# Prompt attention of an NSA step on one core: scores in plain fp32, two heads on the halves of the rows, keys and values kept on chip

## The chip, the core and the metric

The kernel runs on one core of a Trainium2 chip. The metric is device time in microseconds (us); it is given as the median of three runs. The engines are called by the profile's names: PE is TensorE (PEld its weight loads), DVE is VectorE, ACT is ScalarE, POOL is GpSimd, and SP is SyncE, which here only issues DMAs. Each engine has its own queue and takes its instructions in the order of the program.

## What is computed

The program is one inference step of a small decoder trunk: a gated short-convolution layer, then one layer of native sparse attention (NSA) with three branches (compressed, selected, window), then the output projection. It does this for a prompt of 512 new tokens, and for 8 sample rows of one new token each, which read 2,048 cached tokens per row by pages. There are 16 heads of 64, in 4 groups of 4 that share keys and values (4 KV heads). For each query and each branch:

```python
def masked_softmax(s, mask):
    s = jnp.where(mask, s, NEG)
    e = jnp.exp(s - jnp.max(s, axis=-1, keepdims=True)) * mask
    return e / jnp.maximum(jnp.sum(e, axis=-1, keepdims=True), 1e-30)
...
p_win = masked_softmax(scores(qg, win_kv[:, 0], 'qhgd,nhd->qhgn'), w_mask[:, None, None, :])
o_win = jnp.einsum('qhgn,nhd->qhgd', p_win.astype(q.dtype), win_kv[:, 1])
...
o = g[..., 0:1] * o_cmp + g[..., 1:2] * o_sel + g[..., 2:3] * o_win
```

For the prompt all 512 keys of the selected and of the window branch are scored under a causal mask (in tiles of 128 queries, so that query tile qt sees 128·(qt+1) keys), and 32 compressed keys besides. The output o is multiplied by a gate z and projected with a 1024x1024 matrix.

## The kernel before

The program runs in stages on the one core. To 650 us it computes the convolution layer, while PE is busy nearly all the time. Then come the shared keys and values (to 692), the queries (`q_steps`, with the compression of the prompt's keys, to 752), the gates z and the key and value projections (`kvz_steps`), mixed with the key side of the sample rows (to 934), and the attention (935 to 1192), with a tail to 1202.

**The attention.** `attention` (L926) draws steps from two generators. `prompt_steps` (L956) runs over 16 tiles (kvh, qt): 4 KV heads by 4 query tiles. For each tile `prompt_scores` (L1004) makes the scores, their masked maximum (a DVE reduce, L1050), the exponential (ACT, L1053) and a scaling by gate over sum (POOL, L1068), and `prompt_values` (L1076) transposes the probabilities on PE (L1110), evicts them by ACT (L1114) or DVE (L1112) into `pt`, and multiplies by the values (L1101). The second generator, `side`, is the value half of the sample rows (`sample_values`, matmuls at L1335): per page of 128 cached tokens it needs 128 KB, which SP fetches with a register load (L1372) and a DMA (L1377), into two rings of buffers named `kt` and `skv`; 128 pages and some larger loads in all (window rows L1395, `vc_scratch` L1342). When the tiles of the last KV head begin (`last_head`), what is left of `side` is emitted, and from there the output projection (`out_steps`, matmuls L114 to L116, and L1460/L1461 for the sample rows) takes its place. This sets only the order in which the program is written. A scheduler that simulates the engines then moves instructions within it, so PE's final order is its result; the order of SP's queue is fixed by hand.

**Number formats.** A product of two fp32 numbers is made in three fp32r passes (high by high, high by low, low by high) in most stages, so operands are split into a high and a low part. In `q_steps` each head's query is split by one ACT copy (L896) and one DVE subtraction (L897) into QA or QB [128, 2, 4, 512], where the two halves of the 128 rows hold high and low parts. The scores of one head are two accumulated fp32r matmuls over 128 rows (L1043) against KK, which holds a key and its copy on both row halves, high and low as two planes.

**Keys and values on the way.** `kv_prep` (L799) makes, for each branch and KV head, a doubled copy `kd` of the keys (POOL, L805), 4 transposes (L809), a split, and a 512 KB write to `kk_scratch` in DRAM (POOL's queue, L812); the values go to `vt_scratch` (L816). `prompt_head` (L990) loads them again per KV head: VA once (L999, 1 MB), KK for each head (L1002, 1 MB), and copies the 32 compressed keys into place (L1001).

**PSUM.** Eight banks: transposes draw from a ring of two pairs (`tr` and `tx`, two buffers each), the scores have `s` with two buffers, and `acc0` and `acc1` take sums. For the output projection `acc1` and the `tx` pair are used in turn (`psum_o`, L1399).

Of the kernel before, what the change touches and what calls it, by code (L numbers as in the profile page):

```python
# [18 lines left out]
KT = 8  # L19
# [59 lines left out]
class Yoco:  # L79
# [480 lines left out]
    def w1_prep(self):  # L560
# [29 lines left out]
        self.KKd = nc.dram_tensor("kk_scratch", (4, 128, 2, 1024), F32, kind="Internal").ap()  # L590
        self.VTd = nc.dram_tensor("vt_scratch", (128, 2, 1024), F32, kind="Internal").ap()
# [33 lines left out]
    def compress_tail(self, acc, c, n, b):  # L625
# [18 lines left out]
        if c == 0:  # L644
# [4 lines left out]
            if b is None:  # L649
                self.split(self.KC[:, 0], self.KC[:, 1], p3)  # L650
            else:
                kc = cp.tile([128, 2, 128], F32, name="kc", bufs=1)
                for o in range(2):
                    nc.scalar.activation(kc[o * 64:(o + 1) * 64],
                                         p3[o * 64:(o + 1) * 64].rearrange("p (a o) n -> p a o n", o=2)[:, :, o, :],
                                         AF.Copy)
                nc.sync.dma_start(self.KCd[b], kc)
        else:
# [4 lines left out]
            if b is None:  # L663
                p3 = ps[:n, :256].rearrange("p (h d) -> p h d", d=64)

                nc.vector.tensor_copy(self.VC[0:32], p3)
                for o in range(1, 4):
                    nc.gpsimd.tensor_copy(self.VC[o * 32:o * 32 + 32], self.VC[0:32])
# [6 lines left out]
    def kv_init(self):  # L675
# [3 lines left out]
        self.VC = self.slot("VC", [128, 4, 64], F32, "kx1")  # L679
        self.KC = self.slot("KC", [128, 2, 4, 32], F32R, "kx2")  # L680
# [35 lines left out]
    def kv_work(self, br, c, wt):  # L716
# [10 lines left out]
        else:  # L727
            CD = self.kvp.tile([128, 4, 256], F32, name="kvt", bufs=2)
# [70 lines left out]
    def kv_prep(self, br, c, kvt):  # L799

        nc = self.nc
        if c == 0:
            for kvh in range(4):
                kd = self.kvp.tile([128, 4, 2, 64], F32, name="kd", bufs=1)
                nc.gpsimd.tensor_copy(kd, kvt[:, :, kvh * 64:kvh * 64 + 64][:, :, None, :].to_broadcast([128, 4, 2, 64]))  # L805
                yield
                ps = self.psum1()
                for t in range(4):
                    nc.tensor.transpose(ps[:, t * 128:(t + 1) * 128], kd[:, t].rearrange("p u d -> p (u d)"), self.ident)  # L809
                st = self.kvp.tile([128, 2, 512], F32R, name="st", bufs=2)  # L810
                self.split(st[:, 0], st[:, 1], ps)
                nc.gpsimd.dma_start(dram(self.KKd, kvh * 128 * 2048 + (2 - br) * 512, [[2048, 128], [1024, 2], [1, 512]]),  # L812
                                    st.bitcast(F32))
                yield
        else:
            nc.gpsimd.dma_start(self.VTd[:, br - 1], kvt.rearrange("p t n -> p (t n)"))  # L816
            yield
# [56 lines left out]
    def q_steps(self):  # L874
        nc = self.nc
        I = self.I

        QA = self.hp.tile([128, 2, 4, NT], F32R, name="QA", tag="hT")
        QB = self.slot("QB", [128, 2, 4, NT], F32R, "gr1")
        self.QK = [QA[:, 0], QA[:, 1], QB[:, 0], QB[:, 1]]  # L880
        self.QS = self.keep.tile([128, KT, NS], F32, name="QS")
        two = lambda ap: ap.rearrange("p (a n) -> p a n", a=2)
        for hp in range(2):
            for gp in range(2):
                wt = self.wsplit(self.qz_load(0, hp, gp), "norm_b")
                for g2 in range(2):
                    ps = yield from self.product(wt, g2, 128)
                    g = gp * 2 + g2
                    q = self.slot("q", [128, T], F32, "kx%d" % (3 + g2))
                    nc.vector.tensor_tensor(two(q), ps, two(self.RB), op=ALU.mult)  # L890
                    nc.gpsimd.tensor_copy(self.QS[:, hp * 4 + g, :], q[:, NT:])
                    for h2 in range(2):
                        a = slice(h2 * 64, h2 * 64 + 64)
                        o = slice(64 - h2 * 64, 128 - h2 * 64)
                        QK = self.QK[hp * 2 + h2]
# [57 lines left out]
    def psum_s(self):  # L953
        return self.px.tile([128, 512], F32, name="s", bufs=2)

    def prompt_steps(self):  # L956

        tiles = [(kvh, qt) for kvh in range(4) for qt in QORD]
        prev = None
        self.done = []  # L960
        heads = {}
        ahead = self.prompt_head(0, heads)
        for i, (kvh, qt) in enumerate(tiles):
            if qt == QORD[0]:

                for _ in ahead:
                    yield
                self.last_head = kvh == 3
            elif qt == QORD[1] and kvh < 3:
                ahead = self.prompt_head(kvh + 1, heads)  # L970
            H = heads[kvh]
            P = []
            scores = self.prompt_scores(H, kvh, qt, P)
            if prev:

                acc = 0
                for k, _ in enumerate(self.prompt_values(*prev)):
                    acc += SF * 4 / (2 * tiles[i - 1][1] + 3)
# [3 lines left out]
                    if k % 2 and qt != QORD[0]:  # L982
                        next(ahead, None)
# [3 lines left out]
            prev = (heads[kvh], kvh, qt, P)  # L987
# [3 lines left out]
    def prompt_head(self, kvh, heads):  # L991
        nc = self.nc
        at = self.pr

        KK = at.tile([128, 2, 1056], F32R, name="KK", bufs=2)
        heads[kvh] = KK
        if kvh == 0:
            self.VA = at.tile([128, 2, 4, 256], F32, name="VA")
# [4 lines left out]
        yield  # L1003

    def prompt_scores(self, H, kvh, qt, P):
        nc = self.nc
        at = self.pr
        KK = H
# [4 lines left out]
        QK = self.QK[kvh][:, :, qs]  # L1013
        st = at.tile([128, 3, 4, 3], F32, name="pst", bufs=2)
        mx, l, f = st[:, 0], st[:, 1], st[:, 2]
        PC = at.tile([128, 4, 32], F32, name="PC", bufs=3)
        apart = qt in CA
        if apart:
            psc = self.psum1()
            for g in range(4):  # L1020
                for s in range(2):
                    nc.tensor.matmul(psc[:, g * 32:g * 32 + 32], QK[:, g], KK[:, s, 0:32], start=s == 0, stop=s == 1)
            for g in range(4):
                nc.vector.tensor_tensor_reduce(out=PC[:, g], in0=psc[:, g * 32:g * 32 + 32], in1=CM, scale=-SCALE,
                                               scalar=1e28, op0=ALU.add, op1=ALU.min, accum_out=mx[:, g, 0:1])
        for g in range(4):
            pw = self.psum_s()
            ranges = []
            if apart:
                win = pw[:, :W]  # L1030
                ranges += [(win, slice(32, 32 + W))]
            else:
                win, cmp_ = pw[:, 32:32 + W], pw[:, 0:32]
                ranges.append((pw[:, :32 + W], slice(0, 32 + W)))
# [474 lines left out]
```

## Time and profile before

| | us |
|---|---|
| median of 3 runs | 1199.39 (1198.85 to 1204.46) |
| profiled execution, its own time | 1204.16 |
| its span, first to last instruction | 1202.4 |
| PE busy in the span | 1143.7 (95%) |
| attention, 935 to 1192 | 257 |
| PE busy in 935 to 1076, of 141 | 122.8 |
| PE busy in 1076 to 1192, of 116 | 111.8 |

A stage is read by asking which wait ends last in it. A high busy share of PE over the whole span says only that most stages are bound by PE; the attention has two halves that differ, and the last matmul of the sample rows' side (1076) lies between them.

### The profile page before, as it was taken

The numbers are of one execution on the slowest core, as the hardware profiler recorded it, in microseconds if no ns is written. First come the engines' busy times: TensorE is split into PE (matmuls) and PEld (weight loads), VectorE is DVE, ScalarE is ACT, GpSimd is POOL, SyncE is SP. The second block draws the span as 40 slices with busy tenths as digits, with TensorE's granted clock in tenths as the row PEclk, the third lists the DMA queues.
The fourth block names the chain that finished last, engine by engine and source line by source line (L and its number), as shares of the span: only waits on it lengthen the run. The fifth ranks groups of instructions, "written<-read, shape, count | busy, mean of one in ns | idle before, by whom it ended". The sixth has DMA issues, their size and how long they took to land. (4 is left out here: it accounts for less than half of the span.)

```text
span 1202.4 us, 23306 instructions
## 1 busy us (share of the span) xinstructions
PE 1143.7 (95%) x9002; PEld 1023.1 (85%) x9002; DVE 645.3 (54%) x1454; ACT 548.1 (46%) x1096; POOL 266.1 (22%) x373
## 2 busy tenths in 40 slices
PE   6899999999999999999999999989899699899996
PEld 5899999999999999999999999868788455456676
DVE  5545464465544555545548376534345367676832
ACT  6344343353343533435347374433346365566631
POOL 5210310211102111012103001010100355555641
PEclk9899999999999999999999999999999799899999
DMA  7563663665435745448332624587883657665001
GB/s 204 175 195 113 196 210 108 197 198 162 141 115 158 245 132 164 126 130 267 122 124 45 176 45 132 161 271 194 248 204 102 222 172 222 186 202 219 20 36 71
DMA packets 160208, 192.71 MB, mean 160 GB/s; under 512 B 48001, under 2 KB 139497, under 8 KB 159321
## 3 DMA queue, kind: packets, MB, share of 16 engines
q1 hardware_dynamic: 122784, 125.03, 34.5%
q0 software_dynamic: 12112, 44.10, 11.1%
q10 hardware_dynamic: 25200, 22.09, 6.2%
q8 instruction: 71, 1.16, 0.4%
q14 instruction: 41, 0.33, 0.1%
HBM read 167.92 MB, written 31.70 MB: 166 GB/s over the span
## 5 line engine op out<-in xcount | busy, mean ns | idle before, releaser
L114 PE MATMUL mm<-X,wh 128*128 128x260 f32 (+1 forms) x1008 | 291.8, 290 | 3.8 <-ACT wh L103 2.7
L116 PE MATMUL mm<-X,wh 128*128 128x260 f32 (+1 forms) x1008 | 287.8, 286 | 0.5 <-DVE X L360 0.5
L115 PE MATMUL mm<-X,wl 128*128 128x260 f32 (+1 forms) x1008 | 288.1, 286 | 0.0
L114 PEld LDWEIGHTS mm<-X,wh 128*128 128x128 f32 (+1 forms) x1008 | 190.4, 189 | 7.2 <-ACT wh L103 2.9
L116 PEld LDWEIGHTS mm<-X,wh 128*128 128x128 f32 (+1 forms) x1008 | 190.5, 189 | 3.8 <-DVE X L360 0.7
L115 PEld LDWEIGHTS mm<-X,wl 128*128 128x128 f32 (+1 forms) x1008 | 190.7, 189 | 3.1
L603 POOL DMA_INDIRECT G<-in_cache_cmp_kv,cidx x64 | 63.1, 987 | 317.5 <-ACT Gp L609 163.3
L100 ACT ACTIVATE th<-tr 128x512 fp32r<-128x512 f32 x128 | 71.4, 593 | 101.7 <-PE tr L615 101.5
L101 DVE TENSOR_TENSOR tl<-tr,th 128x512 fp32r<-128x512 f32 x128 | 84.1, 683 | 50.0 <-ACT th L100 49.9
L1053 ACT ACTIVATE pp<-pp,pst 128x128 f32<-128x128 f32 (+3 forms) x128 | 70.9, 556 | 39.2 <-DVE pst L1050 37.3
L1068 POOL TENSOR_SCALAR pp<-pp,pst,gt 128x128 f32<-128x128 f32 (+3 forms) x128 | 77.1, 616 | 37.5 <-ACT pp L1053 18.6
L115 PE MATMUL mm<-X,wlx 128*128 128x260 f32 x288 | 82.2, 285 | 0.0
L114 PE MATMUL mm<-X,whx 128*128 128x260 f32 x288 | 81.9, 284 | 0.0
L116 PE MATMUL mm<-X,whx 128*128 128x260 f32 x288 | 81.9, 284 | 0.0
L615 PE MATMUL tr<-ident,Gp 128*128 128x128 f32 x512 | 70.5, 273 | 0.0
L101 DVE TENSOR_TENSOR wl<-wraw,wh 128x1024 fp32r<-128x1024 f32 x38 | 49.5, 1308 | 37.6 <-ACT wh L100 37.3
L1050 DVE CUSTOM_DVE_ANT_0 pp<-s,c_mw 128x128 f32<-128x128 f32 (+3 forms) x128 | 59.0, 484 | 14.1 <-PE s L1043 9.4
L100 ACT ACTIVATE wh<-wraw 128x1024 fp32r<-128x1024 f32 x38 | 39.9, 1056 | 51.6 <-PE mm L116 42.5
L615 PEld LDWEIGHTS tr<-ident,Gp 128*128 128x128 f32 x512 | 59.4, 141 | 1.9
L115 PEld LDWEIGHTS mm<-X,wlx 128*128 128x128 f32 x288 | 54.5, 189 | 2.0
L116 PEld LDWEIGHTS mm<-X,whx 128*128 128x128 f32 x288 | 54.7, 190 | 1.5
L114 PEld LDWEIGHTS mm<-X,whx 128*128 128x128 f32 x288 | 54.6, 190 | 1.4
(421 smaller groups left out, 2733.6 us busy)
## 6 DMA issues: line engine op xcount, KB each, us to landing
skv<-in_cache_sel_kv SPq DMA_DIRECT2D x172, 128.0 KB
wraw<-in_conv_w_in SPq DMA_DIRECT2D x16, 1024.0 KB
wrawx<-in_conv_w_in SPq DMA_DIRECT2D x16, 1024.0 KB
kt<-in_cache_sel_kv SPq DMA_DIRECT2D x84, 128.0 KB
wo<-wo_scratch SPq DMA_DIRECT2D x4, 2048.0 KB
out_win_kv_s<-in_cache_win_kv ACTq DMA_DIRECT2D x8, 1022.0 KB
wrawx<-in_conv_w_out SPq DMA_DIRECT2D x4, 1024.0 KB
wraw<-in_conv_w_out SPq DMA_DIRECT2D x4, 1024.0 KB
```

The source lines that it names most:

```text
L100: nc.scalar.activation(hi, src, AF.Copy)
L101: nc.vector.tensor_tensor(lo, src, hi.bitcast(F32), op=ALU.subtract)
L114: mm(out, sh, mh, start=first, stop=False)
L115: mm(out, sl, mh, start=False, stop=False)
L116: mm(out, sh, ml, start=False, stop=last)
L603: nc.gpsimd.indirect_dma_start(out=G.rearrange("p i c d -> p (i c d)"), out_offset=None, in_=table, in_offset=bass.IndirectOffsetOnAxis(ap ...
L615: nc.tensor.transpose(ps[:, h * 128:(h + 1) * 128], Gp[:, c * 4 + h, :], self.ident)
L1050: nc.vector.tensor_tensor_reduce(out=d, in0=src, in1=m, scale=-SCALE, scalar=1e28, op0=ALU.add, op1=ALU.min, accum_out=mx[:, g, i:i + 1])
L1053: nc.scalar.activation(d, d, AF.Exp, scale=-1.0, bias=mx[:, g, i:i + 1], accum_out=l[:, g, i:i + 1])
L1068: nc.gpsimd.tensor_scalar(P[g2][:, i, :W], P[g2][:, i, :W], f[:, g2, i + 1:i + 2], gates[:, g2, i + 1:i + 2], op0=ALU.mult, op1=ALU.mult)
```

## The change

- Queries stay in plain fp32, in one tile Q with the two heads of a pair (two KV heads, h2 = 0 and 1) on rows 0 to 63 and 64 to 127; the high and low split of Q goes, and with it the separate copy QS of the sample rows' queries.
- Keys likewise: two transposes groups per branch (one per pair of KV heads), evicted straight into KK in SBUF. The values go straight into VA in SBUF. Both scratch tensors in DRAM, their writes and their loads go.
- A step of scores is now two fp32 matmuls over 64 rows each, one per head of the pair, written behind one another (`side_by_side`), into two PSUM banks of one tile of two banks. `s` has two such tiles, four banks; the transposes' ring falls to the two buffers of `tr`.
- The 16 units are (hp, gp, qt): pair of KV heads, half of the group, query tile. Each has 4 (query) heads as before, but two of each KV head. The value products become four matmuls of 256 columns for each t instead of two of 512, the compressed values' are two of 256 columns; the merge `ot` becomes two copies and additions of 64x256 and one POOL multiply of 128x256.
- In the output projection the second and third bank in turn are the two banks of an `s` tile; all four weight tiles `wo` have buffers in one pool; `zs` has a tile of its own.

```diff
 def kv_prep(self, br, c, kvt):
-        if c == 0:
-            for kvh in range(4):
-                kd = self.kvp.tile([128, 4, 2, 64], F32, name="kd", bufs=1)
-                nc.gpsimd.tensor_copy(kd, kvt[:, :, kvh * 64:kvh * 64 + 64][:, :, None, :].to_broadcast([128, 4, 2, 64]))
...
-                nc.gpsimd.dma_start(dram(self.KKd, kvh * 128 * 2048 + (2 - br) * 512, [[2048, 128], [1024, 2], [1, 512]]),
-                                    st.bitcast(F32))
...
+        for hp in range(2):
+            ps = self.psum1()
+            for t in range(4):
+                nc.tensor.transpose(ps[:, t * 128:(t + 1) * 128], kvt[:, t, hp * 128:hp * 128 + 128], self.ident)
+            k = self.KK[:, hp, 32 + (2 - br) * 512:544 + (2 - br) * 512]
+            if hp:
+                nc.vector.tensor_copy(k, ps)
+            else:
+                nc.scalar.activation(k, ps, AF.Copy)
...
 def q_steps(self):
-                    nc.vector.tensor_tensor(two(q), ps, two(self.RB), op=ALU.mult)
-                    nc.gpsimd.tensor_copy(self.QS[:, hp * 4 + g, :], q[:, NT:])
...
-                        nc.scalar.activation(QK[a, g], q[a, :NT], AF.Copy)
-                        nc.vector.tensor_tensor(QK[o, g], q[a, :NT], QK[a, g].bitcast(F32), op=ALU.subtract)
+                    nc.vector.tensor_tensor(two(self.Q[:, hp * 4 + g, :]), ps, two(self.RB), op=ALU.mult)
...
 def attention(self, side):
-        self.ring = [(self.ps, "tr", 2), (self.px, "tx", 2)]
+        self.ring = [(self.ps, "tr", 2)]
...
 def psum_s(self):
-        return self.px.tile([128, 512], F32, name="s", bufs=2)
+        t = self.px.tile([128, 2, 512], F32, name="s", bufs=2)
+        return [t[:, 0], t[:, 1]]
...
-        tiles = [(kvh, qt) for kvh in range(4) for qt in QORD]
+        units = [(hp, gp, qt) for hp in range(2) for gp in range(2) for qt in QORD]
...
-            nc.gpsimd.dma_start(self.VA.rearrange("p b t n -> p b (t n)"), self.VTd)
-        for s in range(2):
-            nc.vector.tensor_copy(KK[:, s, 0:32], self.KC[:, s, kvh, :].bitcast(F32))
-        nc.gpsimd.dma_start(KK[:, :, 32:].bitcast(F32), self.KKd[kvh])
...
+    def side_by_side(self, todo):
+        first = None
+        for out, w, x, start, stop in todo:
+            with ExitStack() as st:
+                if first:
+                    st.enter_context(self.tc.issue_after(first.ins))
+                    st.enter_context(self.tc.high_priority())
+                m = self.nc.tensor.matmul(out, w, x, start=start, stop=stop)
+            first = first or m
...
-                for s in range(2):
-                    nc.tensor.matmul(out, QK[:, g], KK[:, s, cs], start=s == 0, stop=s == 1)
+            for h2 in (1, 0):
+                a = slice(h2 * 64, h2 * 64 + 64)
+                todo.append((outs[h2], self.Q[a, hp * 4 + gp * 2 + g2, qs], self.KK[a, hp, cs], True, True))
+            self.side_by_side(todo)
...
+                for b, h2 in ((1, 0), (0, 0), (0, 1), (1, 1)):
+                    kvh = hp * 2 + h2
+                    c = slice(h2 * 256, h2 * 256 + 256)
+                    todo.append([acc[b * 64:b * 64 + 64, c], self.VA[:, b, t, kvh * 64:kvh * 64 + 64], pt[:, b, c],
+                                 t == top and h2 == 0, False])
...
-        nc.scalar.activation(t1[a], acc[o], AF.Copy)
-        nc.vector.tensor_tensor(t1[a], acc[a], t1[a], op=ALU.add)
-        sz = self.SZ[a, hp * 4:hp * 4 + 4, qs]
-        nc.gpsimd.tensor_tensor(sz, sz, t1[a].rearrange("p (g n) -> p g n", g=4), op=ALU.mult)
+        for h2 in range(2):
...
+            nc.scalar.activation(t1[a], acc[o, c], AF.Copy)
+            nc.vector.tensor_tensor(t1[a], acc[a, c], t1[a], op=ALU.add)
+        nc.gpsimd.tensor_tensor(sz, sz, t1.rearrange("p (g n) -> p g n", g=2), op=ALU.mult)
```

The change also moves instructions on PE. In the fences a row is a line of the kernel, the operation, out<-in by the program's names, and the shape. First PE's order at the start of the attention, before: L1335 is a group of the side, L1022 and L1043 are scores of the compressed keys and of the others, L1110 a transpose of probabilities.

```order
L1335 MATMUL acc_10887<-skv,PT 32x256 x4
L1326 MATMUL tr<-ident,S 8x128
L1022 MATMUL tr<-KK,QA 128x32 x8
L1335 MATMUL acc_10887<-VN,PT 32x256 x4
L1043 MATMUL s<-KK,QA 128x160 x2
L1043 MATMUL s<-KK,QA 128x128 x2
...
L1043 MATMUL s<-KK,QA 128x256 x8
L1110 MATMUL tx<-ident,pp_10930 128x128
L1335 MATMUL acc_10887<-kt,PT 32x256 x8
```

The same place after the change, where L1327 is the side's group, L981 the scores, L1073 and L1112 transposes:

```order
L1327 MATMUL acc_10769<-skv,PT 32x256 x4
L1327 MATMUL acc_10769<-VN,PT 32x256 x4
L981 MATMUL s<-KV,Q 128x160 x2
L981 MATMUL s<-KV,Q 128x128 x2
...
L981 MATMUL s<-KV,Q 128x256 x8
L981 MATMUL s<-KV,Q 128x416 x2
L1327 MATMUL acc_10769<-kt,PT 32x256 x8
L1073 MATMUL tr<-ident,PC 128x128
L1112 MATMUL tr<-ident,pp_10806 128x128
```

The scores no longer name a tile that a DMA fills (KK is now a part of KV, written on chip), and the first `kt` group of the side stands behind more scores. The second place is the end of the side on PE, before; L1101 is a value product, and the last rows are the last group of the side and what follows it.

```order
L1101 MATMUL acc_12814<-pt,VA 64x512 x2
L1335 MATMUL acc_10887<-kt,PT 32x256 x8
L1043 MATMUL s<-KK,QB 128x384 x2
...
L1335 MATMUL acc_10887<-kt,PT 32x256 x4
L1335 MATMUL acc_10887<-skv,PT 32x256 x4
L1110 MATMUL tr<-ident,pp_12848 128x128 x2
L1043 MATMUL s<-KK,QB 128x512 x2
```

And after the change, where the last `kt` and `skv` rows are again the side's last group:

```order
L1327 MATMUL acc_10769<-kt,PT 32x256 x8
L1112 MATMUL tr<-ident,pp_12169 128x128
...
L981 MATMUL s<-KV,Q 128x256 x2
L1327 MATMUL acc_10769<-kt,PT 32x256 x4
L1327 MATMUL acc_10769<-skv,PT 32x256 x4
L981 MATMUL s<-KV,Q 128x256 x4
...
L1354 MATMUL acc_12447<-c_sel,S 128x32 x2
L981 MATMUL acc_12362<-pt,KV 64x256 x8
L1112 MATMUL tr<-ident,pp_12169 128x128
```

The side's last group has moved ahead in PE's order: behind it stood 132 transposes of probabilities (L1110) before, and 180 (L1112) now, of 320 in both; SP's queue has the same order in both.

## Rows read from the trace of the kernel before

**Rows 1.** Span and mean granted clock of the core.
```profile
core 0: 1202.4 us, clock 0.978
```

**Rows 2.** Windows: stretch, length, busy time (instructions) of PE, PEld, DVE, ACT, POOL, clock, DMA share, GB/s.
```profile
692.00:752.00 60.00, 60.00 (x516) 59.82 (x513) 42.73 (x100) 35.88 (x82) 5.25 (x17) 1.00 0.32 89
752.00:935.00 183.00, 171.67 (x1554) 149.78 (x1551) 79.92 (x169) 76.06 (x146) 12.08 (x19) 0.98 0.67 194
935.00:1076.00 141.00, 122.81 (x889) 73.45 (x891) 89.59 (x426) 78.65 (x245) 72.70 (x123) 0.90 0.67 212
1076.00:1192.00 116.00, 111.75 (x790) 87.22 (x782) 66.97 (x233) 58.23 (x169) 59.45 (x79) 0.99 0.23 88
1040.00:1046.00 6.00, 3.66 (x25) 2.38 (x26) 0.65 (x2) 0.07 (x1) 2.19 (x5) 0.50 0.73 220
```

**Rows 3.** Waits of PE in 935 to 1077: total us, times, longest.
```profile
PE s L1043 <- DMA KK<-kk_scratch: 9.7, 1, 9.7
PE acc L1335 <- DMA skv<-in_cache_sel_kv: 6.0, 3, 4.4
PE acc L1335 <- DMA kt<-in_cache_sel_kv: 1.0, 1, 1.0
PE s L1043 <- DVE pst L1065: 0.8, 1, 0.8
```

**Rows 4.** Timeline of SP's queue: start, length of the group's issues, instructions.
```profile
935.89 7.27 SPq L1377 DMA_DIRECT2D kt<-in_cache_sel_kv  x8
943.68 5.22 SPq L1377 DMA_DIRECT2D skv<-in_cache_sel_kv  x4
950.08 6.76 SPq L1377 DMA_DIRECT2D kt<-in_cache_sel_kv  x8
...
996.00 0.39 SPq L1395 DMA_DIRECT2D kt<-in_cache_win_kv  x1
...
998.10 1.17 SPq L1342 DMA_DIRECT2D skv<-vc_scratch  x1
...
1026.41 6.30 SPq L1377 DMA_DIRECT2D kt<-in_cache_sel_kv  x8
1033.23 2.87 SPq L1377 DMA_DIRECT2D skv<-in_cache_sel_kv  x4
1036.67 6.67 SPq L1377 DMA_DIRECT2D kt<-in_cache_sel_kv  x8
...
1057.07 0.94 SPq L1395 DMA_DIRECT2D kt<-in_cache_win_kv  x2
```

**Rows 5.** Chain of waits in the attention: start, us, what.
```profile
998.10 9.69 DMA skv<-vc_scratch
...
1035.76 6.54 DMA skv<-in_cache_sel_kv
1042.34 1.93 PE acc L1335 x16
...
1091.34 0.61 ACT pt L1114
...
1092.68 0.70 DVE pt L1112
```

**Rows 6.** Timeline of PE: start, us, line, tile, shape.
```profile
1074.37 1.03 PE L1101 MATMUL acc<-pt,VA 128*64 128x512 f32 x4
1075.33 0.33 PE L1110 MATMUL tx<-ident,pp 128*128 128x128 f32 x1
...
1075.70 0.64 PE L1335 MATMUL acc<-kt,PT 128*32 128x256 f32 x8
1076.15 0.61 PE L1335 MATMUL acc<-skv,PT 128*32 128x256 f32 x8
1076.70 0.44 PE L1110 MATMUL tr<-ident,pp 128*128 128x128 f32 x2
...
1079.83 0.71 PE L1043 MATMUL s<-KK,QB 128*128 128x512 f32 x2
1080.37 0.60 PE L1110 MATMUL tr<-ident,pp 128*128 128x128 f32 x4
1080.90 1.08 PE L1101 MATMUL acc<-pt,VA 128*64 128x512 f32 x4
...
1191.60 0.28 PE L115 MATMUL tx<-wo,skv 128*128 128x256 f32 x1
1191.72 0.29 PE L116 MATMUL tx<-wo,pt 128*128 128x256 f32 x1
```

**Rows 7.** Lines that go or change: engine, operation, count, ns min/median/max, first and last start.
```profile
L809 PE MATMUL tr<-ident,kd x24: 270/272/328, 778.0 to 857.9; 128*128 128x128 f32 x24
...
L809 PE MATMUL acc<-ident,kd x8: 271/272/273, 842.6 to 847.8; 128*128 128x128 f32 x8
...
L896 ACT ACTIVATE QA<-q x8: 619/628/633, 696.9 to 717.3; 64x512 fp32r<-64x512 f32 x8
...
L1137 DVE TENSOR_TENSOR ot<-acc,ot x16: 672/688/695, 969.9 to 1158.8; 64x512 f32<-64x512 f32 x16
...
L1136 ACT ACTIVATE ot<-acc x16: 577/591/597, 968.2 to 1158.2; 64x512 f32<-64x512 f32 x16
```

More of the change, by code (lines that the diff above doesn't have):

```diff
@@ L727, in kv_work @@
         else:
[L728 removed]
+            CD = self.VA[:, br - 1] if c else self.kvp.tile([128, 4, 256], F32, name="kvt", bufs=2)
             self.kvt = CD
@@ L1012, in prompt_scores @@
         CM = self.cst["cm"][:, qt * 32:qt * 32 + 32]
-        QK = self.QK[kvh][:, :, qs]
         st = at.tile([128, 3, 4, 3], F32, name="pst", bufs=2)
         mx, l, f = st[:, 0], st[:, 1], st[:, 2]
+        gates = self.gt[:, qt, hp * 24:hp * 24 + 24].rearrange("p (h g b) -> p g h b", h=2, b=3)[:, gp * 2:gp * 2 + 2]
         PC = at.tile([128, 4, 32], F32, name="PC", bufs=3)
         apart = qt in CA
-        if apart:
-            psc = self.psum1()
-            for g in range(4):
-                for s in range(2):
[L1022 to L1025, printed above, removed]
@@ new lines, in exps, with compressed @@
+        def exps(d, i, b):
+            nc.scalar.activation(d, d, AF.Exp, scale=-1.0, bias=mx[:, i, b:b + 1], accum_out=l[:, i, b:b + 1])
+        def compressed():
+            nc.gpsimd.tensor_tensor(PC, PC, mx[:, :, 0:1].to_broadcast([128, 4, 32]), op=ALU.subtract)
+            nc.scalar.activation(PC, PC, AF.Exp, scale=-1.0)
+            nc.vector.tensor_reduce(l[:, :, 0], PC, axis=AX.X, op=ALU.add)
+        if apart:
+            psc = self.psum_s()
+            for g2 in range(2):
+                pair([x[:, g2 * 32:g2 * 32 + 32] for x in psc], g2, slice(0, 32))
+            for g2 in range(2):
+                for h2 in range(2):
+                    largest(PC[:, g2 * 2 + h2], psc[h2][:, g2 * 32:g2 * 32 + 32], CM, g2 * 2 + h2, 0)
+            compressed()
@@ new lines, in prompt_scores @@
+        for g2 in range(2):
+            ii = (g2 * 2, g2 * 2 + 1)
+            ps = self.psum_s()
+            b = 0 if apart else 32
+            pair([x[:, :b + W] for x in ps], g2, slice(32 - b, 32 + W))
+            if qt < 2:
+                pair([x[:, b + W:b + 2 * W] for x in ps], g2, slice(544, 544 + W))
+                sel = [x[:, b + W:b + 2 * W] for x in ps]
+            for h2 in range(2):
+                P.append(at.tile([128, 2, 384 + 128 * (qt % 2)], F32, name="pp%d" % (qt % 2), bufs=4))
+            for h2, i in enumerate(ii):
+                largest(P[i][:, 1, :W], ps[h2][:, b:b + W], MW, i, 2)
+                exps(P[i][:, 1, :W], i, 2)
+                if not apart:
+                    largest(PC[:, i], ps[h2][:, :32], CM, i, 0)
+            yield
+            if qt >= 2:
+                sel = [x[:, :W] for x in self.psum_s()]
+                pair(sel, g2, slice(544, 544 + W))
+            for h2, i in enumerate(ii):
+                largest(P[i][:, 0, :W], sel[h2], MW, i, 1)
+                exps(P[i][:, 0, :W], i, 1)
+            if g2 == 1 and not apart:
+                compressed()
+            last = g2 == (0 if apart else 1)
+            gs = slice(ii[0], ii[1] + 1)
+            for r, b in [(gs, slice(1, 3))] + ([(slice(0, 4), slice(0, 1))] if last else []):
+                nc.vector.tensor_scalar(f[:, r, b], l[:, r, b], 1e-30, None, op0=ALU.max)
+                nc.vector.reciprocal(f[:, r, b], f[:, r, b])
+            for h2, i in enumerate(ii):
+                for b in range(2):
+                    nc.gpsimd.tensor_scalar(P[i][:, b, :W], P[i][:, b, :W], f[:, i, b + 1:b + 2],
+                                            gates[:, g2, h2, b + 1:b + 2], op0=ALU.mult, op1=ALU.mult)
+            if last:
+                f4 = f.rearrange("p (g h) b -> p g h b", g=2)[:, :, :, 0]
+                nc.vector.tensor_tensor(f4, f4, gates[:, :, :, 0], op=ALU.mult)
+                nc.gpsimd.tensor_tensor(PC, PC, f[:, :, 0:1].to_broadcast([128, 4, 32]), op=ALU.mult)
+            if g2 == 1:
@@ L1088, in burst @@
         def burst(last):
[L1090 to L1102 removed]
+            todo = []
+            for t, pt in reversed(ready):
+                for b, h2 in ((1, 0), (0, 0), (0, 1), (1, 1)):
[3 more added lines that the diff above has]
+                                 t == top and h2 == 0, False])
+            if last:
+                todo[4:4] = [[acc[h2 * 64:h2 * 64 + 64, h2 * 256:h2 * 256 + 256], self.VC[:, hp],
+                              pb[:, h2 * 256:h2 * 256 + 256], False, False] for h2 in range(2)]
+                todo[-1][4] = todo[-2][4] = True
+            self.side_by_side(todo)
             ready.clear()
```

199 lines of the change are left out of this document (62 added, 137 removed).

## The prediction

> **What bounds the kernel now.** I read the windows by stage first. In 692 to 752 PE is busy 60.00 of 60.00 us and in 752 to 935 it is busy 171.67 of 183 [rows 2]: these stages are PE's. In the attention the two halves differ. In 935 to 1076 PE works 122.81 of 141 us at a granted clock of 0.90; in 1076 to 1192 it works 111.75 of 116 at 0.99 [rows 2]. The waits of PE name the loss of the first half: 9.7 us once, for KK to come back from DRAM, and 6.0 + 1.0 us for pages of the sample rows' side [rows 3].
>
> SP's queue then tells who sets the side's pace. From 935.89 it issues pages without a pause of note: 12 pages take 1036.67 - 1026.41 = 10.26 us, 0.855 each, and the last loads begin at 1057.07 [rows 4]. The chain of waits runs through such loads more than once, up to the one that PE awaits until 1042.34 [rows 5]. But the side's last group runs on PE at 1075.70 [rows 6], 18.6 us after that last issue: at its end the side is no longer late, PE is. So both are near the bound in the first half: SP hands out pages, and PE has other work between them.
>
> **The change part by part.**
>
> *Scores.* The trace has no fp32 matmul on halves of the rows. The nearest row is a pair of value products, fp32 on halves of the columns: four records (two instructions) of 512 columns from 1074.37 to 1075.33, 0.96 us [rows 6], of which about 0.09 is the change of kind of matmul; 0.87 us for 512 columns, 1.7 ns a column, for two heads. Before, two instructions of 512 columns for one head take 1080.37 - 1079.83 = 0.54 [rows 6], some 0.22 each without the change of kind, so 0.88 for two heads. The long products cost the same; what is saved lies in those of 32 columns, which have a floor of about 0.11 each. Over the whole attention I count 46.0 us of scores before and 39.1 after. If row halves did not run side by side, each pair would cost double; both ends stay for the range, and I take the column halves' price, which is the nearest row.
>
> *Values, transposes, projection.* By counts in PE's order and these prices: values 45.0 before and 41.9 after, transposes 36.6 in both (336 at 0.109, from four between 1080.37 and 1080.90 less a change of kind, rows 6), the side 18.3 in both, the projection 51.9 in both (448 at 0.116 to 0.12, rows 6), changes of kind 123 before and 153 after, 11.3 and 14.1 us. Sum: 209.1 before, 201.9 after, so PE has 7.2 us less to do.
>
> *KK and VA stay on chip.* The wait of 9.7 us [rows 3] goes. What is late next there is the pages: the first eight are issued only from 935.89 [rows 4], since SP's queue goes through the constants first, which take their place when the last projection matmul is done. The loads of KK and VA also share the DMA engines with the first pages: eight take 7.27, four 5.22, eight 6.76 us, against 6.30, 2.87 and 6.30 later [rows 4], 3.8 us in all. These come back to SP.
>
> *Key and value preparation.* 32 transposes (24 + 8, rows 7) become 16: 16 x 0.109 = 1.7 us of PE in a stage with PE busy 94% [rows 2]; with the writes to DRAM gone I put the start of the attention 2 us earlier (0 to 6).
>
> *Queries.* 16 ACT splits of 0.628 us [rows 7] and as many on DVE go from a stage in which PE has no idle time [rows 2]: nothing. Merging `ot` takes 32 instructions of 256 columns on ACT and on DVE where 16 of 512 took 0.591 and 0.688 us [rows 7]; at most that much more again, 9.5 and 11 us spread over the 257, at least nothing. Off the path while PE has work: I take nothing, and up to 3 us for the range.
>
> *Where the order puts the side.* This decides. From the first score to the last group of the side, PE's order held 105.3 us of work before, and holds 79.6 now; behind that group it held 103.8 and now holds 122.2. The terms behind it, before: 138 transposes 15.0, scores 14.8, values 17.7, projection 51.9, 37 changes of kind 3.4, the group 1.0. After: 188 transposes 20.5, scores 17.2 (9,600 columns of pairs and a floor for the short ones), values 24.9, projection 51.8, 75 changes 6.9, the group 1.0. PE reads its queue in order, so it can't take the later work while a page is missing.
>
> When do the pages come? SP starts at 935.9 - 2 = 933.9. To the last loads it needs 1057.07 - 935.89 = 121.2 us, less 3.8 (bounds: 113.3, twice that gain, and 121.2): they are issued at 1051.3. Those are 2 MB of window rows; 2.5 MB of the same kind took from 996.00 to 1007.79 (998.10 + 9.69), 11.8 us [rows 4, 5], so 2 MB take 9.4. The last group runs at about 1060.7 (1054 to 1064.5). By its own work PE would be there at 935 + 79.6 x 1.12 = 1024, so it waits some 36 us in the stretch for pages: the 9.7 us are not gained but waited in other places.
>
> Behind it, before, 103.8 us of work took 1191.9 - 1075.7 = 116.2 us [rows 6], 1.12 times as much (waits for evictions, and the rest of the clock). With the same factor 122.2 take 136.8. PE ends at 1060.7 + 136.8 = 1197.5, against 1192.0 (1191.72 + 0.29, rows 6): 5.5 us later. The tail from there to 1202.4 [rows 1] and the 1.8 us around the span stay. The profiled execution goes from 1204.2 to 1209.7; it lies 4.8 over the median, which I take along: the median goes from 1199.4 to 1204.9.
>
> **The rivals.**
>
> *A. The side does not pace PE.* Then the savings arrive: 9.7 + 7.2 x 1.12 + 2 = 19.8 us, 1179.6. For it: the side ends 18.6 us behind SP's last issue before. Against: the spacing of SP's issues, which the change leaves as it is, and the waits for pages that PE has already before, with more work between the groups.
>
> *B. The waits are not lost.* While PE waits for pages, ACT, DVE and POOL finish what is before them, so behind the last group PE finds its inputs ready and the factor falls to 1.02: 122.2 x 1.02 = 124.6, the end at 1185.3, 6.7 us earlier, 1192.7; with T at 1054 or 1064.5 it is 1186 to 1196.5. For it: PE in 1076 to 1192 waits only 4 us outright [rows 2]. Against: the buffers of probabilities are few, so the engines can't run far ahead, and a PE that waits works slower afterwards: the clock in 1040 to 1046, behind the 4.4 us wait, is 0.50 [rows 2, 3].
>
> *C. Row halves do not run side by side as column halves do.* The 17.2 us of scores behind the last group then cost up to double: + 17.2, near 1222. The change would not do what it says. It decides from the point at which a pair of 512 columns takes over 0.95 us. No row of before speaks for or against it.
>
> The Trainium skill, "TensorE: Matmul & The Clock Gate", Part 3 (Measured speedup vs the span model) gives 3.07 times for four products on quarters of the rows, instead of 4. Applied to two halves as an estimate, a pair takes 1.30 times the ideal; that would add 17.2 x 0.30 x 1.12 = 5.8 us, so about 1211. The trace's column groups agree with full overlap rather than with this: 8 instructions of 256 columns, four at a time, from 1075.70 to 1076.70 in 1.00 us [rows 6].
>
> *D. Fewer banks.* The transposes' ring falls from four banks to two. With evictions of 0.61 and 0.70 us [rows 5] on two engines against 0.44 for four transposes, each of the 47 groups of four behind the last side group could wait 0.17: 0 to 8 us; and stretches at half clock behind the page waits 2 to 4 more: 1207 to 1217.
>
> **How the numbers follow.** My forecast has 0.50, with its own range of 1198 to 1210 (the bounds of T, and the factor at 1.10 to 1.14); A has 0.13, B 0.17, C and D together 0.20 (C at its full price 0.05). 0.5% is 6 us, about what a measurement of this kernel can tell from no change: faster is under 1193.4, slower over 1205.4. The forecast lies near that upper border: 0.30 same and 0.20 slower. A is faster, B 0.13 faster and 0.04 same, C and D slower. Together: faster 0.26, same 0.34, slower 0.40. The range leaves out A and the full price of C, under 2 in 10: 1186 to 1220.
>
> **What would show it.** PE's waits of the new trace in the first half: no KK, and instead some 30 us in many waits of the side's line for pages; SP's issues still at 0.855 us a page, ending about 1051; the last group of the side at 1054 to 1065 instead of 1075.7; behind it some 137 us to PE's end. If that group came later than 1065, or the stretch behind it took 125 us, I was wrong, by A or D for the first and by B for the second. For C, a pair of scores of 512 columns has to be near 0.87 us. What would make it wrong above all is a page stream faster than SP's issues of before show.

## The result, and the profile after

The changed kernel takes 1212.67 us (median of 7 runs, 1209.16 to 1215.55), the kernel before 1201.14 (7 runs). The ratio is 1.0091, with a 95% interval of 1.0065 to 1.0117: slower by 11 us. The forecast was 1204.9, which is 5.5 over the 1199.4 that it started from.

The windows of the changed kernel, cut where its stages end: the queries, the stage of z and the keys, the attention up to the side's last group, and from there to PE's end. Columns as in [rows 2].

```profile
692.00:752.00 60.00, 60.00 (x515) 59.75 (x513) 31.29 (x85) 26.79 (x69) 1.08 (x4) 1.00 0.33 89
752.00:927.60 175.60, 166.57 (x1530) 146.47 (x1531) 75.41 (x163) 72.51 (x140) 0.00 (x0) 0.99 0.61 172
927.60:1057.52 129.92, 99.09 (x833) 54.26 (x832) 69.16 (x346) 63.40 (x204) 54.15 (x99) 0.88 0.59 179
1057.52:1203.30 145.78, 132.80 (x1012) 99.47 (x1011) 85.75 (x320) 75.63 (x226) 65.14 (x97) 0.98 0.21 80
```

The first line bears out "nothing" for the queries: the stage is PE's, busy 60.00 of 60 us as before, though DVE, ACT and POOL have less to do there. The second ends 6.8 us earlier than before. The third is the stretch that waits: PE works 99 of 130 us. The fourth, behind the side, has 132.80 us of work where the kernel before had 111.75 in 116 [rows 2]. The waits of PE in 925 to 1100 name the third line's loss, where [rows 3] had KK:

```profile
PE acc L1327 <- DMA kt<-in_cache_sel_kv: 12.0, 5, 3.9
PE acc L1327 <- DMA skv<-in_cache_sel_kv: 11.6, 4, 4.1
PE s L981 <- DVE pst L1006: 7.1, 8, 2.0
PE acc L981 <- DVE pt L1114: 2.5, 3, 1.3
```

L1327 is the side's matmul. The timeline of SP's queue, to be held against [rows 4]:

```profile
929.10 6.36 SPq L1369 DMA_DIRECT2D kt<-in_cache_sel_kv  x8
935.97 3.04 SPq L1369 DMA_DIRECT2D skv<-in_cache_sel_kv  x4
939.60 6.72 SPq L1369 DMA_DIRECT2D kt<-in_cache_sel_kv  x8
...
1015.19 6.41 SPq L1369 DMA_DIRECT2D kt<-in_cache_sel_kv  x8
1022.12 2.86 SPq L1369 DMA_DIRECT2D skv<-in_cache_sel_kv  x4
1025.55 6.68 SPq L1369 DMA_DIRECT2D kt<-in_cache_sel_kv  x8
...
1046.53 0.94 SPq L1387 DMA_DIRECT2D kt<-in_cache_win_kv  x2
```

Twelve pages still take 1025.55 - 1015.19 = 10.36 us. From the first page to the last loads it is 1046.53 - 929.10 = 117.4 us, as forecast. The timeline of PE at the side's last group and at its own end, where [rows 6] had 1075.70 and 1191.72:

```profile
1057.52 0.64 PE L1327 MATMUL acc<-kt,PT 128*32 128x256 f32 x8
1057.98 0.61 PE L1327 MATMUL acc<-skv,PT 128*32 128x256 f32 x8
1058.53 1.13 PE L981 MATMUL s<-KV,Q 64*128 64x256 f32 x8
1059.59 1.09 PE L1112 MATMUL tr<-ident,pp 128*128 128x128 f32 x8
...
1203.43 0.28 PE L116 MATMUL s<-wo,pt 128*128 128x256 f32 x1
```

The side ends 18.2 us earlier than before, and PE 11.7 us later: 146.2 us lie between the two, where 116.3 lay before. The time went into the stretch behind the side: 20.75 us more of busy PE than before (132.80 against 112.05 from 1075.70 on), and some 9 us more of waiting.

### The profile page after: what moved, and what is told of

Read it like the earlier page. It is cut to its first block, busy times and chain, and to the rows that moved or that the text cites. A ratio compares the mean times of both kernels' runs of the same rounds, so it can differ in the third digit from the quotient of the medians.

```text
span 1212.9 us, 23500 instructions
## 1 busy us (share of the span) xinstructions
PE 1136.0 (94%) x9154; PEld 1012.6 (83%) x9154; DVE 628.3 (52%) x1440; ACT 537.3 (44%) x1093; POOL 237.3 (20%) x339
## 5 line engine op out<-in xcount | busy, mean ns | idle before, releaser
L1010 ACT ACTIVATE pp<-pp,pst 128x128 f32<-128x128 f32 (+3 forms) x128 | 70.4, 550 | 36.4 <-DVE pst L1006 34.9
L981 PE MATMUL s<-KV,Q 64*128 64x256 f32 (+6 forms) x320 | 56.2, 467 | 9.8 <-DVE pst L1006 9.5
L1112 PEld LDWEIGHTS tr<-ident,pp 128*128 128x128 f32 x320 | 35.5, 144 | 25.6 <-issue 13.6
```

Source lines behind the costliest of these rows:

```text
L981: m = self.nc.tensor.matmul(out, w, x, start=start, stop=stop)
L1010: nc.scalar.activation(d, d, AF.Exp, scale=-1.0, bias=mx[:, i, b:b + 1], accum_out=l[:, i, b:b + 1])
L1112: nc.tensor.transpose(ps[:, c:c + 128], P[i][:, b, t * 128:(t + 1) * 128], self.ident)
```

## The experiments

In the names, after_ and hold28_ are made from the changed kernel, before_ from the kernel before. Two readings were set against each other. Theory 1: the pages set when the side ends, and PE's order decides how much is left behind it. Theory 2: the new attention waits more on its banks and on DVE, wherever the side stands. The expectations count PE's work by slightly higher prices for short matmuls than the prediction did (82.9 and 125.4 us before and behind the last group in place of 79.6 and 122.2). Each ratio is against runs of the kernel before beside it (medians 1197.6 to 1201.1). The last two columns come from the profiled execution.

| kernel | us | ratio to before (95%) | last side group | behind it, us |
|---|---|---|---|---|
| before | 1201.1 | 1 | 1075.7 | 116.3 |
| changed | 1212.7 | 1.0091 (1.0065 to 1.0117) | 1057.5 | 146.2 |
| after_hold28 | 1191.8 | 0.9944 (0.9914 to 0.9974) | 1064.4 | 118.7 |
| after_hold40 | 1216.9 | 1.0160 (1.0112 to 1.0208) | 1056.4 | 148.6 |
| after_poolc | 1205.1 | 1.0058 (1.0032 to 1.0084) | 1043.4 | 152.1 |
| after_static | 1198.8 | 0.9985 (0.9955 to 1.0016) | 1015.1 | 178.3 |
| after_s4 | 1210.7 | 1.0095 (1.0067 to 1.0124) | 1052.4 | 145.2 |
| before_tr2 | 1209.0 | 1.0077 (1.0052 to 1.0101) | 1067.3 | 130.5 |
| before_nokk | 1191.6 | 0.9935 (0.9912 to 0.9959) | 1067.5 | 111.2 |
| hold28_poolc | 1187.3 | 0.9900 (0.9844 to 0.9955) | 1057.3 | 117.2 |
| before_hold28_poolc | 1191.7 | 0.9929 (0.9906 to 0.9953) | 1067.7 | 112.0 |

**The side's place alone.** In the changed kernel each group of the side is tied behind the last prompt scores written before it, and the side gets a smaller share of steps (`RV`, what each step of the prompt adds to a count that draws one step of the side when it is full).

```diff
-RV = 0.4
+RV = 0.28
 def side_by_side(self, todo):
...
             first = first or m
+        self.held = first
...
             def values(t, rhs, after=None):
-                first = after
+                first = after or getattr(self, "held", None)
+                lead = first is not after
...
-                    first = first or m
+                    if lead or not first:
+                        first, lead = m, False
```

> The changed kernel, with one thing altered: each matmul group of the sample rows' side is tied on PE behind the last prompt scores written before it, and the side's share of steps is 0.28 instead of 0.40, so that its last group stands behind 107.9 us of PE's work instead of 82.9 (by counts and measured prices), with 101.1 instead of 125.4 behind it. Theory 1 (the pages pace the side, and what PE's order leaves behind the last page is added): last side group still at 1055 to 1063, behind it 101.1 x 1.19 = 120, PE's end near 1180, time 1184 to 1197. Theory 2 (the stretch behind the side is long because of the banks and the waits for DVE, wherever the side stands): the waits come back, 1207 to 1216.

Measured: 1191.8, with the side's last group at 1064.44 (1055 to 1063 expected) and 118.7 us behind it (120 expected). The waits of PE up to that group show what became of the 24 us of page waits:

```profile
PE s L981 <- DVE pst L1007: 9.9, 8, 1.9
PE acc L1329 <- DMA kt<-in_cache_sel_kv: 1.9, 2, 1.4
PE tr L1113 <- DVE pb L1082: 1.8, 1, 1.8
PE tr L1074 <- ACT pt L1117: 1.7, 4, 0.6
PE acc L981 <- DVE pt L1115: 1.6, 3, 0.7
PE acc L1329 <- DMA skv<-in_cache_sel_kv: 0.8, 1, 0.8
```

2.7 us for pages are left. Nothing was removed from the kernel; the same work, in another order, is 21 us faster. So theory 2's forecast, that the loss comes back wherever the side stands, failed. Its waits are still there, though: L981 on DVE above, and behind the side's last group PE is idle 10.5 us of 118.7, where the kernel before has 4.2 of 116.3 and the changed kernel 13.0 of 145.8. The control has the tie with the old share.

> Control: the same tie of the side's groups to the prompt's scores, but with the share of 0.40 as in the changed kernel; 81.9 us of PE's work before the last side group and 128.1 behind it. Theory 1: as the changed kernel, 1209 to 1218. Theory 2: the same. If it were under 1200, the tie itself and not the place of the side's end would be what helps.

Measured: 1216.9, no better than without the tie, and 18.6 us of page waits again:

```profile
PE acc L1329 <- DMA kt<-in_cache_sel_kv: 16.2, 7, 4.0
...
PE acc L1329 <- DMA skv<-in_cache_sel_kv: 2.4, 1, 2.4
```

So it is not the tie: the two runs differ in the share alone, and with it in PE's order, which has 128.1 us of work behind the side's end here and 101.1 there.

**Earlier pages.** In the changed kernel SP waits 21.5 us for room for two mask constants, and the pages stand behind them. Here POOL's queue loads these constants.

```diff
-                self.nc.sync.dma_start(t, dram(self.I["consts"], o, [[NCONST, p], [1, w]]))
+                q = self.nc.gpsimd if nm in ("mw", "cm") else self.nc.sync
+                q.dma_start(t, dram(self.I["consts"], o, [[NCONST, p], [1, w]]))
```

> The changed kernel with the loads of the two mask constants (c_mw, c_cm) on POOL's queue. In the changed kernel SP waits 21.5 us for the room of these two, and all pages stand behind them. Theory 1: pages start before 929, by as much as their buffers are free (5 to 20 us), and end by 1027 to 1042; the last side group comes at 1038 to 1052; PE's order leaves 130.8 us behind it, times 1.19 is 156: end 1194 to 1208, time 1204 to 1218 if the order eats it again, at best 1198. Theory 2: no change of the stretch behind, 1207 to 1216. The page waits of PE (24 us in the changed kernel) should fall by half or more by theory 1.

Measured: 1205.1. The pages run from 911.36, the side's last group comes 14.1 us earlier (1043.4), and 152.1 us lie behind it, 5.9 more than in the changed kernel: the scheduler put the side ahead again (130.8 us of work behind its end by the counts, 125.4 in the changed kernel), so about 8 of 14 us remain. The page waits did not halve as I expected; they are 22.0 us (25.0 in the changed kernel). That the order moved along with the pages is my reading of it.

**Pages without SP's pace.**

```diff
-        _, vals = nc.values_load_multi_w_load_instructions(
-            self.ptrow[0:1, at:at + n], engines=[mybir.EngineType.SP], min_val=0, max_val=159,
-            skip_runtime_bounds_check_because="page numbers are rows of the pool")
+        vals = [(at + pg) % 160 for pg in range(n)]
```

> The changed kernel with pages at fixed addresses: SP does no register loads (what is left out: the page table is not read, other pages of the same size are loaded). This takes SP's pace away. PE's order then has 61 us of work before the last side group and 148 behind it. Theory 1: pages no longer take 0.855 us each, the last side group comes at 985 to 1030, PE is bound by its own work and its waits for evictions: 148 x 1.19 = 176 behind it, time 1172 to 1200. Rival (the changed attention is limited by the banks and DVE, pages or not): 1205 to 1216.

Measured: 1198.8, at the edge of theory 1's range. SP's timeline shows the pace gone, 4 pages in 1.86 us where it took 2.86:

```profile
924.65 3.70 SPq L1367 DMA_DIRECT2D kt<-in_cache_sel_kv  x8
928.39 1.86 SPq L1367 DMA_DIRECT2D skv<-in_cache_sel_kv  x4
930.66 4.57 SPq L1367 DMA_DIRECT2D kt<-in_cache_sel_kv  x8
...
1003.20 1.08 SPq L1385 DMA_DIRECT2D kt<-in_cache_win_kv  x1
```

What went is the load of each page's number into a register, in the changed kernel:

```profile
L1364 SPq TENSOR_LOAD <-ptrow x192: 267/279/928, 752.8 to 1045.6; - x192
```

The side ends 42 us earlier and 32 of these come back behind it: the order has only 61 us of work before the side's end now, and 148 behind it. So fast pages alone don't give the savings; an order that fills their gaps gives more.

**Banks.** Two kernels change the banks here, and two more on a later base. The scores' banks singly, in the changed kernel:

```diff
-        t = self.px.tile([128, 2, 512], F32, name="s", bufs=2)
-        return [t[:, 0], t[:, 1]]
+        return [self.px.tile([128, 512], F32, name="s", bufs=4) for _ in range(2)]
```

> The changed kernel with the four score banks allocated singly (four buffers of one bank) instead of two pairs, so that a head's bank is free after its own reduction. Nearly the same PE order by counts (85.0 before the last side group, 124.6 behind). Theory 1: pages still pace it, last side group at 1055 to 1062; if the waits of scores on DVE (7.1 us in 925 to 1100, 6.7 behind the side) come from the pairs, they shrink by half and the time is 1206 to 1211; if they come from the reductions' own pace, 1210 to 1216.

Measured: 1210.7; its ratio of 1.0095 is that of the changed kernel. The waits of scores on DVE in 925 to 1100 did fall, from 7.1 to 4.8 us, and PE's idle time behind the side from 13.0 to 8.4 us, but the time can't be told from the changed kernel's. The run doesn't clear the pairs, for its edit does a second thing: with single banks the two heads' products often no longer run side by side. A head alone then takes as long as a pair does, as two rows of this run show (x2 is one product of 512 columns, x4 a pair):

```profile
1074.88 1.12 PE L980 MATMUL s<-KV,Q 64*128 64x512 f32 x2
...
1076.53 1.13 PE L980 MATMUL s<-KV,Q 64*128 64x512 f32 x4
```

PE is busy 68.93 us with the scores of this run, and 56.19 with those of the changed kernel (both in 920 to 1210). What single banks save in waits, they lose in overlap. In the kernel before, the transposes on two banks:

```diff
-        self.ring = [(self.ps, "tr", 2), (self.px, "tx", 2)]
+        self.ring = [(self.ps, "tr", 2)]
```

> The kernel before with one part of the change alone: the transposes of the attention draw from two banks instead of four. Its PE order puts the last side group behind 98.8 us of work instead of 111.5 and leaves 118.0 instead of 107.4 behind it. Theory 1: last side group at 1062 to 1070 (loads as before), then 118 x 1.12 to 1.19 = 132 to 140: 1203 to 1218. Theory 2 (banks cost by waits for evictions in place): last side group near 1075.7 as before, and 0 to 8 us more behind it: 1200 to 1209; the waits of transposes on ACT and DVE show it.

Measured: 1209.0. The side's last group came at 1067.3, as theory 1 said, and 130.5 us lie behind it (132 to 140 expected), of which PE works 123.07:

```profile
1067.32:1197.80 130.48, 123.07 (x853) 92.87 (x852) 78.83 (x286) 67.64 (x197) 65.31 (x90) 1.00 0.24 93
```

That is 11.3 us more work than the kernel before has there [rows 2], and 3.2 us more idle time. This one edit moved the side forward in PE's order by itself. Why, no run shows; my reading is that with fewer banks the scheduler finds the prompt's transposes not ready and takes side groups in their stead.

**The wait for KK alone.** In the kernel before, the first KV head's keys are not loaded (zeros set by DVE).

```diff
-        nc.gpsimd.dma_start(KK[:, :, 32:].bitcast(F32), self.KKd[kvh])
+        if kvh:
+            nc.gpsimd.dma_start(KK[:, :, 32:].bitcast(F32), self.KKd[kvh])
+        else:
+            nc.vector.memset(KK[:, :, 32:].bitcast(F32), 0.0)
```

> The kernel before without the first load of KK (what is left out: the first KV head's keys are zeros set by DVE), so the wait of 9.7 us goes. PE's order: 117.0 us of work before the last side group, 102.6 behind it. Theory 1 (the wait is worth its price only where PE, and not the page stream, sets the side's end): here PE has enough work between the pages; last side group at 1062 to 1070, time 1186 to 1194. Rival (the wait comes back as page waits here as well): 1195 to 1202, with page waits of PE over 15 us.

Measured: 1191.6, faster by 8 to 9 us, with the side's last group at 1067.5. That is nearly the price of the wait of 9.7 us [rows 3], and PE waits little for pages in its stead:

```profile
PE acc L1338 <- DMA skv<-in_cache_sel_kv: 3.4, 3, 2.4
PE acc L1338 <- DMA kt<-in_cache_sel_kv: 1.7, 2, 1.3
PE s L1046 <- DVE KK L1001: 1.2, 1, 1.2
```

This fits theory 1. But the edit moved PE's order too (102.6 us of work behind the side's end by the counts, where before_tr2's expectation gives 107.4 for the kernel before), and the stretch behind shrank by 5.1 us. So the run does not separate the wait's price from that of the order.

**A version that beats both.** The tie, the share of 0.28 and the constants on POOL's queue together:

> The changed kernel with the side tied and the share of 0.28, and the constants' loads on POOL's queue besides. 108.4 us before the last side group, 101.1 behind. With the tie alone PE waited only 2.7 us for pages, so theory 1 expects little of earlier pages here: 1186 to 1193, against 1191.8 with the tie alone; the wait at the start for c_mw (1.9 us) should go. If it falls under 1183, pages still pace PE there.

Measured: 1187.3, ratio 0.990. Its windows up to the side's last group and behind it, to be held against the third and fourth line at the top:

```profile
926.00:1057.25 131.25, 120.76 (x1006) 66.23 (x1004) 93.27 (x442) 82.50 (x264) 68.34 (x125) 0.97 0.54 170
1057.25:1174.40 117.15, 106.69 (x843) 85.41 (x841) 64.34 (x223) 55.79 (x166) 52.33 (x74) 0.99 0.23 87
```

In the same time up to the side's end PE works 120.76 us instead of 99.09. Is that the change's merit, or that of the edits? The kernel before with the same ones:

> The kernel before with the same two edits that brought the changed kernel to 0.990: the side's groups tied behind the last prompt scores, share 0.28, and the mask constants on POOL's queue. PE's order: 117.5 us before the last side group, 102.9 behind. Theory 1 (with the order evened out, what the change saves itself is its 9.7 us wait and the 6.8 us of earlier start, less more waits on DVE): the wait for KK stays, last side group at 1070 to 1078, behind it 111: time 1192 to 1200, so the change is worth 5 to 13 us at an equal order. Rival (the gain is that of the tie and the constants alone): 1183 to 1191, as the changed kernel with them.

Measured: 1191.7, ratio 0.9929 (0.9906 to 0.9953), with the wait for KK (10.2 us) still in it. This lies between the two ranges, 0.3 us under that of theory 1 and 0.7 over the rival's. The two intervals overlap: at an even order the change is worth some 4 us at the medians, not 5 to 13, and that it is worth anything is not certain from these runs. The stretch behind the side's last group shows where the rest of the wait's 10.2 us goes, to be held against the second line of the changed kernel above:

```profile
1067.69:1179.72 112.03, 107.63 (x769) 84.70 (x768) 65.98 (x223) 56.32 (x164) 55.12 (x74) 0.98 0.24 91
```

At nearly the same work PE is idle 4.4 us here and 10.5 us in the changed kernel. So theory 2 was wrong about the loss, but some 6 us of waits do belong to the changed attention, wherever the side stands. Three more on the changed kernel's base:

> The changed kernel with the tie, the share 0.28 and the constants on POOL's queue; besides, of the 80 evictions of transposes that DVE makes those of odd t go to ACT. DVE loses some 24 evictions of 0.70 us, ACT gains as many of 0.61. If DVE's load is what makes PE wait in the prompt's attention (11 to 13 us of waits name it), the time falls from 1187 to 1177 to 1184; if the waits are those of the chain through both engines, 1185 to 1192.

```diff
-                if b:
+                if b and t % 2 == 0:
                     nc.vector.tensor_copy(pt[:, b], ps)
```

Measured: 1184.5, ratio 0.9876 (0.9844 to 0.9907): the fastest of all by its median, clear of both kernels, but not told apart from the base at 0.990, and between the two ranges of the expectation.

> The same base as the run with evictions moved, with the four score banks allocated singly instead of in two pairs. In the changed kernel this made no difference against before (1.0095 and 1.0091), where PE waited for pages; here PE's own waits count. If the pairs hold banks too long, 1179 to 1184; if not, 1185 to 1194 (its order has 2.3 us more changes of kind).

Measured: 1185.9, ratio 0.989 (0.985 to 0.993): no difference in time here either, and the same trade. PE's idle time behind the side's last group falls from 10.5 to 3.5 us and its busy time rises from 106.7 to 112.4; its scores take 64.70 us, with pairs 55.19 (both in 920 to 1210).

> The same base with the banks the other way: four for transposes, one pair for scores. Order 113.3 us before the last side group, 95.6 behind. If the transposes' ring of two banks costs more than it gives to the scores, 1178 to 1184; if the scores need their second pair, 1190 to 1205, with longer waits of scores on DVE.

```diff
-        t = self.px.tile([128, 2, 512], F32, name="s", bufs=2)
+        t = self.px.tile([128, 2, 512], F32, name="s", bufs=1)
...
-        self.ring = [(self.ps, "tr", 2)]
+        self.ring = [(self.ps, "tr", 2), (self.px, "tx", 2)]
```

Measured: 1207.6, ratio 1.0079 (1.0051 to 1.0107), 20 us over its base and over both ranges of the expectation. The longest waits of PE in its attention:

```profile
PE s L982 <- DVE pst L1008: 13.0, 15, 3.7
PE tr L1114 <- POOL pp L1058: 3.4, 7, 0.7
PE tr L1075 <- POOL PC L1063: 2.1, 1, 2.1
```

The base waits 8.4 us on that first line. Four banks for transposes and one pair for scores are 20 us slower than two banks and two pairs: the second pair of score banks, for which the change gave up the transposes' second two, is needed.

## Why the prediction was right, and where it was off

The direction and the mechanism came out, the size only in part. The measured 1212.67 lies in the whole range of 1186 to 1220, but 2.7 us over the forecast's own of 1198 to 1210, and inside that of rival D.

**Right, and shown: the place of the side.** The rows of before said that SP hands out pages at 0.855 us and that PE's order had moved its own work behind them. The changed kernel's page waits and the last group at 1057.5 (forecast 1060.7, 1054 to 1064.5) agree, and after_hold28 against after_hold40 differs in the share alone, and so in PE's order, and moves the time by 25 us. That the group came so near its forecast is in part luck: SP began 4.8 us earlier than the 933.9 reckoned with, and from the last loads' issue to the group it took 11.0 us instead of 9.4. In the stretch PE waited 25.0 us for pages, not 36: its own work up to the group took 99.09 us, where the sum had 79.6 x 1.12 = 89. Which edit moved the side: before_tr2 shows, in the kernel before, that halving the transposes' ring is enough to move 11 us of work, of the 20.75 that the whole change moved; what moved the rest was not tried.

**Right: the work behind the side.** PE's busy time there rose from 112.05 us (1075.70 to 1192.00) to 132.80, by 20.75; the sum had 18.4 us of work and 20.6 with its factor.

**Mis-sized: the factor of 1.12.** I let it stand for waits and clock alike, and 122.2 us of work took 146.2, a factor of 1.20. The idle time of PE behind the side is 145.78 - 132.80 = 13.0 us, against 4.2 before. These 8.8 us are most of the 9.4 by which the stretch exceeded the 136.8 of the forecast. The waits of PE there:

```profile
PE s L981 <- DVE pst L1006: 5.6, 6, 1.7
PE acc L981 <- DVE pt L1114: 2.6, 2, 1.4
PE tr L1112 <- DVE pt L1114: 2.0, 5, 0.6
PE s L1454 <- DVE pst L1006: 1.1, 1, 1.1
PE tr L1112 <- ACT pt L1116: 0.9, 2, 0.7
PE s L114 <- ACT pt L108: 0.6, 1, 0.6
```

They are prompt attention's waits, mostly for DVE; the projection, which makes up over 50 us of either stretch, hardly waits. More prompt work behind the side means more of these, so the factor should have been taken for the prompt's part alone. But that explains little: without the projection's 51.9 us the factor was 1.24 before, and 51.8 + 70.4 x 1.24 = 139.1 is only 2.3 us over the forecast's 136.8. The prompt's part itself waits more, by a factor of 1.34, and so it does at an even order, by some 6 us (hold28_poolc against before_hold28_poolc). What makes it wait stays open. Two banks for transposes cost 3.2 us of idle time in before_tr2, moving evictions off DVE changed nothing that can be told, and one pair of score banks less makes it worse. The pairs of score banks remain a candidate: single banks took away 4.6 and 7.0 us of idle time behind the side in the two kernels that have them, and cost as much in busy time, with heads that often no longer ran side by side. No kernel frees the banks singly and keeps the heads together.

**Off: the start.** I put the attention 2 us earlier (0 to 6); it is 6.8 (from 934.40 to 927.60). PE's busy time up to there fell by 4.5 us (171.07 in 752.00 to 934.40 before, 166.57 now), and its idle time by 2.3.

**The rivals.** A (nothing paces PE) falls with the 25 us of page waits. B (the others get ahead, factor 1.02) falls with the factor: it rose. D (fewer banks, 1207 to 1217) named the right size, and in part by luck. Its way, evictions that PE waits for on the spot, shows in before_tr2 with 3.2 us of idle time; the 11 us of work that moved there came through the order, which D did not name. In the changed kernel the waits of transposes on evictions (L1112, above) are 2.9 us of the 13.0. C (row halves not side by side) falls with two pairs of 256 columns in 1059.59 - 1058.53 = 1.06 us, the changes of kind at both ends in it; one after the other the four products would take 4 x 256 x 1.7 ns = 1.74 us. And it falls with the rows of after_s4: 512 columns take 1.12 us for one head and 1.13 for a pair, with the changes of kind in both.

The Trainium skill, "TensorE: Matmul & The Clock Gate", Part 3 (Measured speedup vs the span model), gives 3.07 for four products on quarters of the rows. Applied to halves, as an estimate, those pairs would take 1.30 times as long. The trace doesn't agree for halves: 1.06 us less about 0.2 for two changes of kind is 0.86, the full overlap of 0.87, and the pair of after_s4 takes 1.01 times what one head does.

## What to carry to other kernels

Where a steady stream of loads feeds one of two interleaved streams of work on an engine, compare the stream's end with the work that the order leaves behind it: end of loads plus the work behind is the time, and a wait that is removed earlier is only moved. Count that work in the new order before pricing the edits; an edit of a few PSUM banks can move it by more than the edits save. And when such a change disappoints, set the order by hand before judging it, in the kernel before as well: here the same edits gave the kernel before most of the gain, and some 4 us were left for the change.

## What the runs showed of the hardware

Two fp32 matmuls on the two halves of the rows ran fully side by side: without the changes of kind, two pairs of 256 columns took 0.86 us, and one pair of 512 on halves of the columns 0.87. Pages fetched by their number cost SP's queue more than pages at fixed addresses: four took 2.86 us with the register loads and 1.86 without. Most of the difference is the loads, 0.279 us each (median of 192), and not the address in a register: the DMA instruction itself took 0.333 us with it and 0.430 at a fixed address (medians).
